# Column sums of an 8192 x 8192 matrix: the first block of rows laid out by halves, and three small TensorE sums moved around the second strip

One core of a Trainium2 chip. The metric is the device time of one execution in microseconds, the median over runs.

## The reference

```python
def setup_inputs():
    return {"x": np.random.randn(8192, 8192).astype(np.float32)}   # 268.4 MB

def reference(x):
    return np.sum(x, axis=0)                                        # 8192 numbers
```

## The kernel before

The rows come in 32 blocks of 256 (8 MiB each, two rows per partition). VectorE folds 31 blocks into a running sum. The last block is summed as six parts of its first 128 rows ("halves") and six strips of its other 128 rows, the strips getting narrower. TensorE reduces halves, strips and VectorE's carry over the partitions with a matmul by ones. ScalarE and VectorE copy the sums out of PSUM, and three stores write them.

```python
    G = NBUF * P * K                                   # P 128, K 2, NBUF 3
    xg = x[0 : near // NBUF * G, :].rearrange(
        "(g p b k) c -> g b p k c", p=P, b=NBUF, k=K)  # 30 blocks, interleaved in threes
    xn = x[near * P * K : last * P * K, :].rearrange("(p k) c -> p k c", k=K)
    xl = x[last * P * K :, :].rearrange("(k p) c -> k p c", p=P)
    # ... cut: tiles, semaphores
    def piece_sums(src, n, start, sem=None, val=0):    # 4 matmuls, one per 32 PSUM partitions
    # ... cut
        for t in range(last):
            i = nc.sync.dma_start(out=bufs[t % NBUF][:],
                in_=xn if t == near else xg[t // NBUF, t % NBUF])
            if t >= NBUF:
                i._wait_ge(s_free, t - NBUF + 1)
            i.then_inc(s_buf[t % NBUF], 16)
    # ... cut: two loads of halves, six of strips, each strip with its own semaphore
        half(0, s_half[0])
        half(1)
        carry_sums(0)
        carry_sums(1)
        half(2, s_half[1])
        strip_sums(0)
        strip_sums(1)
        carry_sums(2)
        for n in (3, 4, 5):
            half(n)
        strip_sums(2)
        carry_sums(3)
        strip_sums(3)
        carry_sums(4)
        carry_sums(5)
        strip_sums(4)
        strip_sums(5)
    # ... cut: six copies out of PSUM, three stores
```

Of the kernel before, what the change touches and what calls it, by code (L numbers as in the profile page):

```python
# [10 lines left out]
P = 128  # L11
K = 2
NBUF = 3
# [10 lines left out]
def kernel(  # L24
# [5 lines left out]
    nc = tc.nc  # L30
# [3 lines left out]
    near, last = T - 2, T - 1  # L34
# [1 line left out]



    G = NBUF * P * K
    xg = x[0 : near // NBUF * G, :].rearrange(  # L40
        "(g p b k) c -> g b p k c", p=P, b=NBUF, k=K
    )
    xn = x[near * P * K : last * P * K, :].rearrange("(p k) c -> p k c", k=K)
    xl = x[last * P * K :, :].rearrange("(k p) c -> k p c", p=P)

    pool = ctx.enter_context(tc.tile_pool(name="sb", bufs=1))
# [4 lines left out]
    bufs = [  # L51
        pool.tile([P, K, C], F32, name=f"buf{b}", tag=f"buf{b}") for b in range(NBUF)
    ]
# [19 lines left out]
    def rows(t, k, c0=0, w=None):  # L73
        return bufs[t % NBUF][:, k, c0 : C if w is None else c0 + w]
# [3 lines left out]
    def vadd(o, a, b, sem, val):  # L78

        nonlocal n_dve  # L80
        i = nc.vector.tensor_tensor(out=o, in0=a, in1=b, op=ADD)  # L81
        i._wait_ge(sem, val)
        i.then_inc(s_dve, 1)
        n_dve += 1
        return n_dve

    def piece_sums(src, n, start, sem=None, val=0):

        w, r = STRIPS[n], RUN[n]
        runs = src[:, START[n] : START[n] + w].rearrange(  # L90
            "p (u j i) -> p j u i", j=NJ, i=r
        )
        for j in range(NJ):
            i = nc.tensor.matmul(  # L94
                out=ps[n][32 * j : 32 * j + 32, 0 : w // NJ],
                lhsT=ones[:],
                rhs=runs[:, j],
                start=start,
                stop=True,
                skip_group_check=True,  # L100
            )
            if sem is not None and j == 0:
                i._wait_ge(sem, val)
        return i

    with tc.tile_critical(sync_engine=mybir.EngineType.DVE) as section:  # L106
        nc.gpsimd.memset(ones[:], 1.0).then_inc(s_one, 1)  # L107







        def take(sem, n):
            nc.vector.sem_inc(sem, -n)._wait_ge(sem, n)  # L116

        def block(b):
            r0, r1 = bufs[b][:, 0, :], bufs[b][:, 1, :]
            take(s_buf[b], 17)  # L120
            nc.vector.tensor_tensor(  # L121
                out=r0, in0=r0, in1=bufs[(b - 1) % NBUF][:, 1, :], op=ADD
            ).then_inc(s_op, 1)
            take(s_op, 1)
            nc.vector.sem_inc(s_free, 1)  # L125
            nc.vector.tensor_tensor(out=r1, in0=r1, in1=r0, op=ADD).then_inc(  # L126
                s_buf[(b + 1) % NBUF], 1
            )

        assert near % NBUF == 0  # L130
        take(s_buf[0], 16)
        nc.vector.tensor_tensor(  # L132
            out=rows(0, 1), in0=rows(0, 1), in1=rows(0, 0), op=ADD
        ).then_inc(s_buf[1], 1)
        for b in range(1, NBUF):
            block(b)
        with nc.vector.Fori(0, near // NBUF - 1):
            for b in range(NBUF):
                block(b)


        carry = {}
        for c0, parts in ((0, ((0, 2 * GROUP),)), (2 * GROUP, ((2, GROUP), (3, GROUP)))):
            w = 2 * GROUP
            d = vadd(
                rows(near, 0, c0, w),
                rows(near, 0, c0, w),
                rows(near - 1, 1, c0, w),
                s_buf[near % NBUF],
                17,  # L150
            )
            for g, gw in parts:
                v = vadd(
                    rows(near, 1, g * GROUP, gw),
                    rows(near, 1, g * GROUP, gw),
                    rows(near, 0, g * GROUP, gw),
                    s_dve,
                    d,
                )
                for i in range(gw // GROUP):  # L160
                    carry[g + i] = v


        for t in range(last):
            i = nc.sync.dma_start(out=bufs[t % NBUF][:], in_=xn if t == near else xg[t // NBUF, t % NBUF])
            if t >= NBUF:
                i._wait_ge(s_free, t - NBUF + 1)
            i.then_inc(s_buf[t % NBUF], 16)

        for h in range(2):  # L170
            c0, w = h * (C // 2), C // 2
            i = nc.sync.dma_start(out=rows(last, 0, c0, w), in_=xl[0][:, c0 : c0 + w])  # L172
            if h == 0:
                i._wait_ge(s_free, last - NBUF + 1)
            i.then_inc(s_half[h], 16)
        for n, w in enumerate(STRIPS):
            c0 = START[n]
            nc.sync.dma_start(  # L178
                out=rows(last, 1, c0, w), in_=xl[1][:, c0 : c0 + w]
            ).then_inc(s_strip[n], 16)  # L180



        def half(n, sem=None):
            piece_sums(rows(last, 0), n, True, sem, 16)

        def carry_sums(n):
            piece_sums(rows(near, 1), n, False, s_dve, carry[min(n, 3)])

        def strip_sums(n):  # L190
            piece_sums(rows(last, 1), n, False, s_strip[n], 16).then_inc(s_pe, 1)

        nc.tensor.wait_ge(s_one, 1)
# [3 lines that stand above are left out]
        carry_sums(1)  # L197
        half(2, s_half[1])
        strip_sums(0)
        strip_sums(1)  # L200
        carry_sums(2)
        for n in (3, 4, 5):
            half(n)
        strip_sums(2)
        carry_sums(3)
        strip_sums(3)
# [6 lines that stand above are left out]
        at = [START[n] // NJ for n in range(len(STRIPS))]  # L213
        for n in range(len(STRIPS)):
            w = STRIPS[n] // NJ
            o, p = res[:, at[n] : at[n] + w], ps[n][:, 0:w]
            c = nc.vector.tensor_copy(out=o, in_=p) if n in (3, 5) else nc.scalar.copy(o, p)  # L217
            c._wait_ge(s_pe, n + 1)
            c.then_inc({3: s_three, 5: s_end}.get(n, s_act), 1)

        lanes = slice(0, 32 * (NJ - 1) + 1, 32)

        def store(eng, n0, n1, sem, val):
            c0, c1 = START[n0], START[n1] + STRIPS[n1]
            return eng.dma_start(
                out=out[c0:c1].rearrange("(u j i) -> j u i", j=NJ, i=RUN[n0]),
                in_=res[lanes, c0 // NJ : c1 // NJ].rearrange(
                    "j (u i) -> j u i", i=RUN[n0]
                ),
            )._wait_ge(sem, val).then_inc(s_out, 16)  # L230

        store(nc.sync, 0, 2, s_act, 3)
        store(nc.sync, 3, 3, s_three, 1)
        nc.sync.wait_ge(s_act, 4)
        store(nc.sync, 4, 5, s_end, 1)
# [42 lines left out]
```

## Time and profile before

| | value |
|---|---|
| time | 627.25 us, median of 3 runs (627.19 to 627.32) |
| span of the profiled execution | 625.6 us (this execution took 627.52) |
| DMA | busy in all slices, 268.44 MB read |
| VectorE | 531.2 us busy, idle for a while in each block |
| TensorE | 13.2 us busy, all of it after 607 us |

The prediction shows the lines. A timeline line gives start, length, engine, source line, operation, names, shapes and count, then in brackets the idle time before it and what ended that. In the listing of transfers the last number is the time from issue to landing.

### The profile page before, as it was taken

To read this page: it belongs to the slowest core of one execution; us is meant where nothing else is said; L and a number is where in the kernel's file an instruction comes from. 1 tells how busy PE (TensorE), PEld (TensorE's weight loads), DVE (VectorE), ACT (ScalarE), POOL (GpSimd) and SP (SyncE) were. 2 spreads that over 40 slices of the span, in tenths; PEclk is the share of its full clock that TensorE was granted. 3 is DMA by queue.
4 is the path that set the end of the run, shared out by engine and by line. 5 is a ranking of instruction groups with operands and counts; after the bars stand their busy time and mean duration, and the time that the engine had idled before them with its cause. 6 is when DMAs were issued, how large, how long until landed. Compare 5 with 4: busy or idle time off the path is not lost. (4 is left out here: it accounts for less than half of the span.)

```text
span 625.6 us, 571 instructions
## 1 busy us (share of the span) xinstructions
PE 13.2 (2%) x144; PEld 4.1 (1%) x144; DVE 531.2 (85%) x66; ACT 3.4 (1%) x5; POOL 0.3 (0%) x5
## 2 busy tenths in 40 slices
PE   0000000000000000000000000000000000000016
PEld 0000000000000000000000000000000000000002
DVE  0538988889888899888898888988889888899887
ACT  0000000000000000000000000000000000000001
POOL 0000000000000000000000000000000000000000
PEclk9999999999999999999999999999999999999999
DMA  9999999999999999999999999999999999999997
GB/s 402 402 469 402 465 406 465 406 465 406 448 423 432 440 419 453 402 469 402 469 402 469 402 469 402 465 406 465 406 465 406 453 419 432 440 423 448 402 435 306
DMA packets 5661, 268.49 MB, mean 429 GB/s; under 512 B 652, under 2 KB 784, under 8 KB 1052
## 3 DMA queue, kind: packets, MB, share of 16 engines
q1 hardware_dynamic: 5660, 268.47, 99.2%
q8 instruction: 1, 0.02, 0.0%
HBM read 268.44 MB, written 0.03 MB: 429 GB/s over the span
## 5 line engine op out<-in xcount | busy, mean ns | idle before, releaser
L121 DVE TENSOR_TENSOR buf<-buf,buf 128x8192 f32<-128x8192 f32 x29 | 252.1, 8693 | 58.1 <-DVEq L116 58.1
L126 DVE TENSOR_TENSOR buf<-buf 128x8192 f32<-128x8192 f32 x29 | 252.1, 8693 | 6.9 <-DVEq L116 6.9
L132 DVE TENSOR_TENSOR buf<-buf 128x8192 f32<-128x8192 f32 x1 | 8.7, 8691 | 23.1 <-DVEq L116 23.1
L94 PE MATMUL ps<-buf,ones 128*32 128x512 f32 (+3 forms) x144 | 13.2, 513 | 609.5 <-DMA buf<-in_x_dram 609.1
L81 DVE TENSOR_TENSOR buf<-buf,buf 128x4096 f32<-128x4096 f32 x2 | 8.8, 4422 | 1.6 <-DMA buf<-in_x_dram 1.6
L81 DVE TENSOR_TENSOR buf<-buf 128x2048 f32<-128x2048 f32 (+1 forms) x3 | 8.9, 3000 | 0.1
L94 PEld LDWEIGHTS ps<-buf,ones 128*32 128x32 f32 x144 | 4.1, 117 | 618.5 <-DMA buf<-in_x_dram 610.9
L217 ACT COPY res<-ps 128x512 f32<-128x512 f32 (+1 forms) x4 | 2.1, 520 | 618.7 <-PE ps L94 618.7
L217 DVE COPY res<-ps 128x256 f32<-128x256 f32 (+1 forms) x2 | 0.7, 325 | 2.0 <-PE ps L94 2.0
L217 ACT ACT_TABLE_LOAD x1 | 1.3, 1283 | 1.0 <-DVEq L106 1.0
L107 POOL MEMSET ones<- 128x32 f32 x1 | 0.1, 126 | 0.6 <-DVEq L106 0.6
L262 POOL MEMSET const-bfloat16-1.0<- 128x1 bf16 x1 | 0.1, 102 | 0.0
L262 POOL MEMSET const-uint8-127<- 128x1 uint8 x1 | 0.1, 102 | 0.0
L262 POOL MEMSET const-float32-0.0<- 128x1 f32 x1 | 0.1, 99 | 0.2 <-issue 0.2
L262 POOL MEMSET const-float32-1.0<- 128x1 f32 x1 | 0.1, 99 | 0.0
## 6 DMA issues: line engine op xcount, KB each, us to landing
buf<-in_x_dram SPq DMA_DIRECT2D x2, 2048.0 KB, 17.5
buf<-in_x_dram SPq DMA_DIRECT2D x3, 1024.0 KB, 23.6
buf<-in_x_dram SPq DMA_DIRECT2D x1, 512.0 KB, 26.4
buf<-in_x_dram SPq DMA_DIRECT2D x31, 29.7
buf<-in_x_dram SPq DMA_DIRECT2D x1, 384.0 KB, 26.8
buf<-in_x_dram SPq DMA_DIRECT2D x1, 128.0 KB, 26.7
out_dram<-res SPq DMA_DIRECT2D x2, 4.0 KB
out_dram<-res SPq DMA_DIRECT2D x1, 24.0 KB
```

What stands on the lines that cost most here:

```text
L81: i = nc.vector.tensor_tensor(out=o, in0=a, in1=b, op=ADD)
L94: i = nc.tensor.matmul(out=ps[n][32 * j : 32 * j + 32, 0 : w // NJ], lhsT=ones[:], rhs=runs[:, j], start=start, stop=True, skip_group_chec ...
L107: nc.gpsimd.memset(ones[:], 1.0).then_inc(s_one, 1)
L121: nc.vector.tensor_tensor(out=r0, in0=r0, in1=bufs[(b - 1) % NBUF][:, 1, :], op=ADD).then_inc(s_op, 1)
L126: nc.vector.tensor_tensor(out=r1, in0=r1, in1=r0, op=ADD).then_inc(s_buf[(b + 1) % NBUF], 1)
L132: nc.vector.tensor_tensor(out=rows(0, 1), in0=rows(0, 1), in1=rows(0, 0), op=ADD).then_inc(s_buf[1], 1)
L217: c = nc.vector.tensor_copy(out=o, in_=p) if n in (3, 5) else nc.scalar.copy(o, p)
L262: nc = _bacc.Bacc("TRN2", target_bir_lowering=False, num_devices=1)
```

## The change

The intent: start the stream with pieces that neighbouring partitions read next to each other, and do the half-row sums of strips 3 to 5 while TensorE waits for strips, not when it is late for strip 2.

```diff
-    G = NBUF * P * K
-    xg = x[0 : near // NBUF * G, :].rearrange(
-        "(g p b k) c -> g b p k c", p=P, b=NBUF, k=K
-    )
-    xn = x[near * P * K : last * P * K, :].rearrange("(p k) c -> p k c", k=K)
+    F = P * K
+    xf = x[0:F, :].rearrange("(k p) c -> p k c", p=P)
+    xg = x[F : last * F, :].rearrange("(g p b k) c -> g b p k c", p=P, b=NBUF, k=K)
...
-            i = nc.sync.dma_start(out=bufs[t % NBUF][:], in_=xn if t == near else xg[t // NBUF, t % NBUF])
+            rows_in = xg[(t - 1) // NBUF, (t - 1) % NBUF] if t else xf
+            i = nc.sync.dma_start(out=bufs[t % NBUF][:], in_=rows_in)
...
         strip_sums(0)
+        half(3)
         strip_sums(1)
+        half(4)
+        half(5)
         carry_sums(2)
-        for n in (3, 4, 5):
-            half(n)
         strip_sums(2)
```

## The prediction

> **What bounds the kernel now.** I read the page's first parts, then the chain of waits that ended last, then the timeline of the last 35 us, then the issue times of the last transfers with their times to landing.
>
> ```profile
> span 625.6 us, 571 instructions
> PE 13.2 (2%) x144; PEld 4.1 (1%) x144; DVE 531.2 (85%) x66; ACT 3.4 (1%) x5; POOL 0.3 (0%) x5
> ...
> DMA  9999999999999999999999999999999999999997
> ...
> L121 DVE TENSOR_TENSOR buf<-buf,buf 128x8192 f32<-128x8192 f32 x29 | 252.1, 8693 | 58.1 <-DVEq L116 58.1
> L126 DVE TENSOR_TENSOR buf<-buf 128x8192 f32<-128x8192 f32 x29 | 252.1, 8693 | 6.9 <-DVEq L116 6.9
> ```
>
> The DMA row is full in 39 of 40 slices. VectorE works 8.69 + 8.69 us per 8 MiB block plus short gaps and then waits (58.1 us over 29 blocks, 10.6 of them before block 1), so it is not the bound. The first L121 add starts at 42.44 and the first L81 add, which the landing of block 30 released, at 602.62: (602.62 - 42.44) / 29 = 19.317 us per 8.389 MB block, or 434 GB/s. The transfer of each block is issued long before it can begin (29.7 us median from issue to landing against 19.3 us of moving), so the queue is never empty between the first packet and the last. Whatever shifts the start of the stream, or lengthens it anywhere, shifts the end by as much. Only two ends are not transfer: the start-up (issue at 0.97, first add at 23.15: 22.18 us, 2.9 us over a block's 19.3) and the tail. The tail in the timeline, from different stretches of it:
>
> ```profile
> 615.88 4.50 DVE L81 TENSOR_TENSOR buf<-buf 128x2048 f32<-128x2048 f32 x2
> ...
> 617.26 5.49 PE L94 MATMUL ps<-buf,ones 128*32 128x512 f32 x96 [1.39 <-DMA buf<-in_x_dram]
> 618.22 0.16 PEld L94 LDWEIGHTS ps<-buf,ones 128*32 128x32 f32 x8 [0.80 <-DVE buf L81]
> ...
> 621.95 0.43 DVE L217 COPY res<-ps 128x256 f32<-128x256 f32 x1 [1.57 <-PE ps L94]
> 622.71 0.32 ACT L217 COPY res<-ps 128x192 f32<-128x192 f32 x1 [1.04 <-PE ps L94]
> 622.82 0.22 DVE L217 COPY res<-ps 128x64 f32<-128x64 f32 x1 [0.45 <-PE ps L94]
> ```
>
> From 617.26 to the end TensorE runs without a break: the 96 matmuls carry no later wait. So at the very end TensorE, not the arrival of data, sets the pace, and it is late against the data. How late comes from the landings of the last strips (numbered 0 to 5):
>
> ```profile
> 593.61 23.61 DMA buf<-in_x_dram
> ...
> buf<-in_x_dram SPq DMA_DIRECT2D x1, 1024.0 KB, 25.6
> buf<-in_x_dram SPq DMA_DIRECT2D x1, 512.0 KB, 26.4
> ...
> buf<-in_x_dram SPq DMA_DIRECT2D x1, 384.0 KB, 26.8
> buf<-in_x_dram SPq DMA_DIRECT2D x1, 128.0 KB, 26.7
> ```
>
> Issues follow each other by 0.475 us: strip 1 at 593.61, strip 2 at 594.08, then 594.55, 595.03 and 595.50 for strips 3, 4 and 5. With 25.6, 26.4, 26.8 and 26.7 to landing: strip 1 lands at 617.22, strip 2 at 619.7, strip 3 at 620.95, strip 4 at 621.83, strip 5 at 622.2. In the timeline strip 2's sums start only at 619.97, strip 3's at 621.26, strip 4's at 622.13 and strip 5's, the last matmuls, at about 622.46. Each is 0.25 to 0.3 us after its landing, where an unblocked start follows a landing by about 0.04 us (617.22 to 617.26).
>
> [...] the last block's two half-row transfers (16 KB pieces) land 4.87 us apart for 2.097 MB (592.66 + 19.7 against 592.29 + 15.2), while a quarter of a 64 KB-piece block takes 19.317 / 4 = 4.83. [...] blocks read at a 192 KB pitch per partition, and the block at 64 KB and the last block at 32 KB, all keep 418 to 437 GB/s.
>
> **The change part by part.**
>
> (a) Order of TensorE in the tail. Nothing is added or removed: 144 matmuls before and after, the same 18 groups. `half(3)` (8 matmuls, 0.43 us) moves in front of strip 1, `half(4)` and `half(5)` (0.32 + 0.11 us) between strip 1 and `carry_sums(2)`. Before, all three (0.86 us, from 619.11 to 619.97) stood between `carry_sums(2)` and strip 2. A 512-column group takes 0.86 us, read from the starts.
> - `half(2)` ends at 614.43, strip 0 starts at 614.81 and its matmuls are fed by 615.7. `half(3)` takes 615.7 to 616.1. Strip 1 lands only at 617.22, so it falls wholly into the 1.39 us idle stretch: free.
> - Strip 1 is fed by 618.12. `half(4)` and `half(5)` take until 618.57. `carry_sums(2)`, which VectorE freed at 618.17 (615.88 + 2.29), starts 0.36 us later than before, and is through at 619.43. Strip 2 lands at 619.7, so this delay is free too.
> - Strip 2 then starts at 619.7 + 0.05 = 619.77 in place of 619.97: 0.20 us gained. From there the order is as before and has no hole if nothing else binds: `carry_sums(3)` at 620.63 (VectorE done at 615.88 + 4.50 = 620.38), strip 3 at 621.06 (landed 620.95), strip 4 at 621.93 (landed 621.83), strip 5 at 622.25 (landed 622.2). All are ready, the last by only 0.05 us. The last matmuls, the two last copies and the last store move 0.20 us earlier with them. More than about 0.21 cannot be had, as strip 5 lands at 622.2.
>
> Sum of (a): -0.20 us.
>
> (b) First block. Before, each partition reads one 64 KB piece; now two 32 KB pieces, 4 MB apart. 128 packets more, 8 more on each of the 16 engines. From the comparison above, 6 more packets per engine cost 4.87 - 4.83 = 0.04 us, so about 0.007 us each (an estimate that charges the extra semaphore write to them as well); 8 of them cost +0.06 us. They delay the whole stream, as it never idles.
>
> (c) Start-up. The issue-to-first-add time has 2.9 us of latency in it[...]. Neighbouring partitions' first pieces were 192 KB apart and will be 32 KB apart. I have no measured basis for a sign and take 0, give or take 0.25 us; it passes to the end in full.
>
> (d) The other 30 blocks shift by 256 rows and the block before the last joins the interleaving. Its interval (583.42 to the landing wait that ended at 602.62, 19.2 us between add starts) is no different from the others, so 0.
>
> VectorE's adds have the same shapes and count; nothing changes there: 0. Total: -0.20 + 0.06 + 0 = -0.14 us, or 627.25 - 0.14 = 627.11, rounded to 627.1.
>
> **The rivals.**
> - The stream's start moves. For it: the 2.9 us of start-up, and that every later landing hangs on it. If the new layout opens faster, up to -0.3 us more: about 626.8. If the 256 smaller pieces delay the first packets, +0.3: about 627.4. This is the largest uncertainty.
> - Address conflict in the first block. [...] Halving the rate in one block would add 19 us: 646. Against it: the last block is read with exactly this row-per-partition pitch at full rate. I give it below 1%.
> - TensorE's gain is swallowed: VectorE frees `carry_sums(3)` at 620.38 and strips 4 and 5 land within 0.1 us of when TensorE would want them. If part (b) makes everything land 0.06 later, the gain over those landings stays the same, since VectorE and strips shift together. If the wait in front of strips 4 or 5 adds a tenth, the gain is 0.1 and the time 627.2.
> - Later delivery of `carry_sums(2)` delays strip 2. Slack is 0.3 us (619.43 against 619.7), so this needs slower matmuls than those of the same minute[...].
>
> **Range and chances.** The measured runs of before lie within 0.13 us. With start-up (0.25), tail (0.1) and the scatter (0.1) taken as independent, the spread is about 0.28, and 8 in 10 needs 1.28 times that, 0.36: 626.7 to 627.5, widened slightly. Two per cent is 12.5 us, out of reach for the tail, and only the address conflict could make it slower by that much.
>
> **What would show it.** Right: one PE break in front of strip 2 with a wait on DMA, near 619.8; strip 5's matmuls within 0.1 us of its landing; 128 more packets; all L119 and L124 adds at 8.69 us; the first VectorE add at 23.2, give or take 0.25. Wrong: a first add outside that, an interval of blocks other than 19.3 us, or a PE break before strips 3 to 5 that eats the 0.20 us.

The charge in (b) is an estimate from the trace's 4.87 and 4.83 us, shared evenly over 16 DMA engines. Even sharing fits the changed kernel's records: 256 pieces of 32 KB, each 1.213 us in the median, make 256 x 1.213 / 16 = 19.4 us, a block's time. What the 2.9 us of the start-up consist of was not shown. The rival of an address conflict is a bare supposition, its halved rate, 646 us and 1% included. What speaks against it is measured: the last block's 8.389 MB took 19.63 us by the records (602.29 to 621.92, the ends of block 30's and strip 5's last 4-byte packets), which is 427 GB/s against the 434 of the blocks before it.

## The result

The changed kernel took 627.54 us (median of 6 runs: 627.22, 627.35, 627.53, 627.55, 628.75, 628.84). The kernel before took 627.29 (6 runs, 627.19 to 627.49). The ratio is 1.0009, with a 95% interval of 0.9996 to 1.0022: the same. Ratios are the mean time of one kernel's fast runs over that of the other's of the same rounds, so not quite the ratio of the medians quoted. The forecast of "within 2%" held. The median lies 0.04 us above the range, and two runs lie 1.3 us above it. All runs counted as fast, as 1.3 us is only 0.2%.

The changed kernel's page shows the same work and 128 packets more:

```profile
span 625.8 us, 571 instructions
...
DMA packets 5789, 268.49 MB, mean 429 GB/s; under 512 B 652, under 2 KB 784, under 8 KB 1052
...
L119 DVE TENSOR_TENSOR buf<-buf,buf 128x8192 f32<-128x8192 f32 x29 | 252.1, 8692 | 58.6 <-DVEq L114 58.6
L130 DVE TENSOR_TENSOR buf<-buf 128x8192 f32<-128x8192 f32 x1 | 8.7, 8693 | 22.9 <-DVEq L114 22.9
```

The first add waited 22.9 us, not 23.1: the stream opened 0.23 us earlier. The tail, from the changed kernel's timeline:

```profile
602.91 4.43 DVE L79 TENSOR_TENSOR buf<-buf,buf 128x4096 f32<-128x4096 f32 x1 [1.57 <-DMA buf<-in_x_dram]
...
620.07 0.16 PEld L92 LDWEIGHTS ps<-buf,ones 128*32 128x32 f32 x8 [1.05 <-DMA buf<-in_x_dram]
...
622.54 0.17 PEld L92 LDWEIGHTS ps<-buf,ones 128*32 128x32 f32 x8 [0.16 <-DMA buf<-in_x_dram]
622.83 0.32 ACT L217 COPY res<-ps 128x192 f32<-128x192 f32 x1 [1.04 <-PE ps L92]
622.94 0.23 DVE L217 COPY res<-ps 128x64 f32<-128x64 f32 x1 [0.45 <-PE ps L92]
```

TensorE now waits for strip 2 (620.07) and for strip 5 (622.54): it is no longer late. (The brackets give the idle time of the weight loads. By the records the break between matmuls before strip 2 is just under 0.15 us, too short for the timeline to print.) The last strip lands at 622.50 (record of the trace) and its first matmul starts at 622.58, 0.08 behind; before it was 622.20 and 622.46, 0.26 behind. From the add that block 30 releases to the last copy it is 622.94 - 602.91 = 20.03 us, against 622.82 - 602.62 = 20.20. But block 30's add itself is 0.29 us later than before. That came in the middle. Three adds of the kernel before:

```profile
100.48 8.69 DVE L121 TENSOR_TENSOR buf<-buf,buf 128x8192 f32<-128x8192 f32 x1 [1.69 <-DVEq L116]
119.77 8.69 DVE L121 TENSOR_TENSOR buf<-buf,buf 128x8192 f32<-128x8192 f32 x1 [1.66 <-DVEq L116]
139.09 8.69 DVE L121 TENSOR_TENSOR buf<-buf,buf 128x8192 f32<-128x8192 f32 x1 [1.70 <-DVEq L116]
```

and the same three of the changed kernel:

```profile
100.36 8.69 DVE L119 TENSOR_TENSOR buf<-buf,buf 128x8192 f32<-128x8192 f32 x1 [1.82 <-DVEq L114]
119.67 8.69 DVE L119 TENSOR_TENSOR buf<-buf,buf 128x8192 f32<-128x8192 f32 x1 [1.69 <-DVEq L114]
139.25 8.69 DVE L119 TENSOR_TENSOR buf<-buf,buf 128x8192 f32<-128x8192 f32 x1 [1.96 <-DVEq L114]
```

The steps are 19.29 and 19.32 before, 19.31 and 19.58 after. VectorE is as fast as ever, and the waits in brackets are longer: the data came late. Over the whole stream, first add to block 30's, it is 579.99 us against 579.47: 0.52 lost. So in the profiled run: -0.23 (start) + 0.52 (stream) - 0.17 (tail) = +0.12 at the last copy. The two profiled executions still took 627.53 and 627.52: at the end of the profiled span the difference is 0.11 (625.75 against 625.64 by the records), so about 0.1 lies outside it, where no trace looks. The sum is good to a tenth at best. This leaves the two runs at 628.8, which the profiled one does not explain.

### The profile page after: what moved, and what is told of

Same layout as the page of the kernel before. It is cut to its first block, busy times and chain, and to the rows that moved or that the text cites. A ratio compares the mean times of both kernels' runs of the same rounds, so it can differ in the third digit from the quotient of the medians.

```text
span 625.8 us, 571 instructions
## 1 busy us (share of the span) xinstructions
PE 13.4 (2%) x144; PEld 3.9 (1%) x144; DVE 531.2 (85%) x66; ACT 3.4 (1%) x5; POOL 0.3 (0%) x5
## 5 line engine op out<-in xcount | busy, mean ns | idle before, releaser
L130 DVE TENSOR_TENSOR buf<-buf 128x8192 f32<-128x8192 f32 x1 | 8.7, 8693 | 22.9 <-DVEq L114 22.9
## 6 DMA issues: line engine op xcount, KB each, us to landing
buf<-in_x_dram SPq DMA_DIRECT2D x1, 384.0 KB, 26.8
buf<-in_x_dram SPq DMA_DIRECT2D x1, 128.0 KB, 26.7
```

The source lines that it names most:

```text
L130: nc.vector.tensor_tensor(out=rows(0, 1), in0=rows(0, 1), in1=rows(0, 0), op=ADD).then_inc(s_buf[1], 1)
```

## The experiments

Sixteen kernels, each timed in 5 rounds, in four groups of four that shared a chip and the runs of the kernel before. All results were correct. "Slow" below means a run over 628 us, split_all aside, whose packets alone cost 1 us. The layout of the change has two parts: "shift" moves the 30 blocks by 256 rows, "split" reads the first block in two pieces per partition.

| run | layout | order | other | five times, sorted, us |
|---|---|---|---|---|
| tail_only | before | new | | 627.07 627.07 627.09 627.13 627.46 |
| shift_only | shift alone | new | | 627.04 627.10 627.13 627.14 628.50 |
| split_only | split alone | new | | 627.07 627.28 628.56 628.76 629.03 |
| both_again | new | new | | 626.93 627.04 627.06 627.28 629.25 |
| after_32_more | new | new | 32 instructions more | 628.42 628.46 628.64 628.65 628.66 |
| before_32_more | before | before | 32 more | 627.12 627.26 627.29 627.55 629.03 |
| after_32_fewer | new | new | 32 fewer | 627.05 627.06 627.23 627.24 627.53 |
| layout_only | new | before | | 627.20 627.21 627.32 627.77 627.78 |
| order_32_fewer | before | new | 32 fewer | 627.24 627.25 627.25 627.30 627.32 |
| fewer_again | new | new | 32 fewer | 627.01 627.06 627.07 627.10 627.51 |
| shift_32_fewer | shift alone | new | 32 fewer | 627.25 627.25 627.26 627.26 627.32 |
| split_all | all split | new | 32 fewer | 628.05 628.14 628.21 628.22 628.77 |
| before_64_more | before | before | 64 more | 628.13 628.34 628.35 628.39 628.98 |
| both_third | new | new | | 627.02 627.20 627.33 628.78 629.14 |
| order_again | before | new | | 626.94 627.30 627.34 627.36 627.38 |
| after_16_fewer | new | new | 16 fewer | 627.05 627.15 627.17 627.17 627.45 |

The kernel before, over all groups: 42 runs, median 627.28, 41 of them from 627.16 to 627.57 and one at 628.91.

### First group: which part of the change

The first theory was that the stretch of slow blocks belongs to the layout (its shift, or its split first block), the rival that it is chance.

tail_only is the kernel before with the TensorE lines of the diff alone:

> Only the new TensorE order, with the row layout of before. In all theories the tail gives its 0.18 to 0.20 us: 627.05 to 627.1 against 627.25, the last strip's matmuls under 0.1 us behind its landing, the first add at 23.15 as before. If the slow stretch between 80 and 200 us of the changed kernel (about 0.5 us lost to block intervals of 19.45 to 19.58 in place of 19.32) belongs to the layout, none of it is seen here, and no run is over 627.5. If it is chance (another kernel's or another chip's noise), block intervals over 19.42 and runs near 628.8 appear here as well.

Measured: median 627.09, no run over 627.5. From block 30's add (602.51) to the last copy (622.53) it is 20.02 us, so the tail's gain is there without the layout. Its stream took 579.48.

shift_only is the changed kernel with

```diff
-    xf = x[0:F, :].rearrange("(k p) c -> p k c", p=P)
+    xf = x[0:F, :].rearrange("(p k) c -> p k c", k=K)
```

> The changed kernel, but the first block with 64 KB pieces, so that only the shift of the interleaved 30 blocks by 256 rows is left of the layout. Theory that the shifted addresses cause the slow stretch: intervals over 19.42 between 80 and 200 us, 627.3 to 627.6, and some runs near 628.8. Theory that the first block's pieces (their start and the offsets between DMA engines that they leave) cause it: intervals of 19.27 to 19.39 throughout, 627.0 to 627.15.

Measured: four runs at 627.04 to 627.14, and no slow stretch beyond 60 us. The shifted addresses are not its cause. But the fifth run took 628.50, and it was the profiled one. Its stream took 579.57, as in the others. The time went in the last two microseconds. TensorE in the timeline, and then the last two strips in the listing of transfers:

```profile
617.10 5.18 PE L92 MATMUL ps<-buf,ones 128*32 128x512 f32 x80 [0.99 <-DMA buf<-in_x_dram]
623.57 0.32 PE L92 MATMUL ps<-buf,ones 128*32 128x64 f32 x8 [1.28 <-DMA buf<-in_x_dram]
...
buf<-in_x_dram SPq DMA_DIRECT2D x1, 384.0 KB, 26.9
buf<-in_x_dram SPq DMA_DIRECT2D x1, 128.0 KB, 28.2
```

Strip 4 took its usual 26.9 us. Strip 5 took 28.2 in place of 26.7, and TensorE sat idle 1.28 us for it. By the records of its landing, fifteen of the sixteen counts of its semaphore, one from each DMA engine as I read it, were in by 622.00 and one at 623.52. For that one, the packet of 4 bytes that counts the semaphore up started only at 622.43. (In the kernel before, the last such packet of strip 5 ends at 621.92, and the last count comes at 622.20.) What held it up is in the queues of the 0.1 us from 621.45 to 621.55 (packets that start there, MB, their time as a share of the 16 engines'):

```profile
q8 instruction: 1, 0.02, 58.2%
q1 hardware_dynamic: 18, 0.02, 44.8%
```

The page calls queue q8 "instruction", and I take what it moves for a fetch of instructions: one packet of 16,384 bytes from 621.51 to 622.44 (0.93 us). The late packet started in its last 0.02 us and ended 0.01 us after it. The records do not name an engine; that the two shared one is read from these times. The fetch's 0.93 us is also not the whole loss: the late packet landed 1.1 us after its start, where the fifteenth took 0.29 (621.71 to 622.00). Every profile here has exactly one such fetch in the tail; the page of before counts it too (queue q8, one packet, 0.0%), and I had passed over it.

In 15 of the 18 profiles taken in all, the fetch did not make the run slow. This run took 1.4 us more than its others. What let the fetch go first, the records do not show.

Offsets between the engines, which the expectation takes to come from the first block's pieces, are in the records of the pair: in the kernel before, the sixteen 4-byte packets of a block (one from each engine, as I read it) end 0.67 to 0.72 us apart, from first to last, in every one of 31 blocks; in the changed kernel 0.39 to 0.52. That it is the pieces that leave them was not shown.

split_only moves the split first block to the rows ahead of the last block, so that the 30 blocks keep their old addresses:

```diff
-    xf = x[0:F, :].rearrange("(k p) c -> p k c", p=P)
-    xg = x[F : last * F, :].rearrange(...)
+    xf = x[near * F : last * F, :].rearrange("(k p) c -> p k c", p=P)
+    xg = x[0 : near * F, :].rearrange(...)
```

> The changed kernel, but the first block takes its rows (in two 32 KB pieces per partition, as in the change) from just ahead of the last block, and the interleaved 30 blocks keep the addresses of before. Theory that the first block's pieces cause the slow stretch: first add about 0.2 us earlier than 23.15, then intervals over 19.42 somewhere in the first 200 us, 627.3 to 627.6 and a scatter of over 1 us. Theory that the shifted addresses cause it: the early first add is kept, intervals 19.27 to 19.39, 626.8 to 626.9.

Measured: three of five runs slow, and the scatter that I had expected, but not for the reason given: the profiled run (627.07) lost only 0.1 us in its stream, and the slow runs' 1.5 to 2.0 us over it are nearer to the 1.4 of the delayed strip than to the 0.5 of a slow stretch.

> The changed kernel itself once more, for its scatter. If the slow stretch is a property of this kernel: median 627.3 to 627.6, at least one run in six over 628, and again block intervals over 19.42 in the first 220 us, perhaps elsewhere than before. If it was chance: median 626.85 to 627.0, no run over 627.3.

Measured: one slow run, and the other four at 626.93 to 627.28. The run at 626.93 was profiled: first add at 22.88, stream 579.47, tail 622.34 - 602.35 = 19.99. That is the predicted course, with both gains and no loss. The slow stretch is thus no fixed property of the kernel.

### Second group: is it the fetch?

The theory now: TensorE's sequencer asks for its next block at a fixed place in its program. The new order brings that place forward against the landings, and now and then the request comes before one DMA engine has taken its last input packets. No record shows the request; this is a guess to be tested. The rivals: chance, the store, or the layout alone. The test changes only how many instructions TensorE has. after_32_more and before_32_more add, to the changed kernel and to the kernel before:

```diff
         nc.tensor.wait_ge(s_one, 1)
+        for _ in range(8):
+            nc.tensor.matmul(out=ps[5][0:32, 0:32], lhsT=ones[:], rhs=ones[:],
+                             start=True, stop=True, skip_group_check=True)
```

> The changed kernel with 8 tiny dummy matmuls ahead of everything on TensorE: 32 instructions more in its program (each fp32 matmul is two weight loads and two passes), done at 1 us, where nothing waits for them. Theory that the slow runs of about 628.5 are made by TensorE's instruction fetch (one 16 KB packet of 0.93 us in the instruction queue) that overtakes the last strip's final packet on one of the 16 DMA engines, and that it is asked for when TensorE reaches a fixed place in its program: the fetch now starts about two groups (0.6 to 0.9 us) earlier, before 621.0, always ahead of that engine's last packets; every run slow, 627.9 to 628.7. Theory that the slow runs have another cause (a late transfer by chance, the store on the same queue): the 32 instructions change nothing, most runs 626.9 to 627.3 and one in three at 628.5.

Measured: five of five slow, 628.42 to 628.66. The fetch started at 621.10, while strip 4 was still coming, and strip 4 landed late as well (28.1 us from issue, against 26.8). A cause by chance or by the store is out: the first store was issued at 621.73, after the fetch. (The dummies were done at 2.24 us rather than 1: TensorE's next matmul, at 607.76, had 605.52 us of idle time before it. Two weight loads and two passes for each matmul call is what the page of before shows: 144 of each for 72 calls.) Nor is it the granted clock: four of these five runs have a mean of 1.000, and so have 11 of the 21 slow runs. (Three of the longer ones have 0.997: 629.03 of before_32_more, 628.98 of before_64_more and 628.91 of the kernel before. There the clock may have added something; no profile shows it.)

> The kernel before with the same 8 dummy matmuls, neither layout nor order changed. Fetch theory: the kernel before gets slow runs as well, though it never had one in 18 runs: at least three of five at 628.0 to 629, the fetch starting earlier than 621.53. If the new layout or the new order itself makes the slow runs: all runs at 627.2 to 627.5 as without the dummies.

Measured: one of five slow (629.03), not three: a miss, and not clear of the one in 42 of the kernel before. The fetch of the profiled run started at 621.38, 0.16 earlier than in the kernel before, and still just after its engine had finished. By the theory, then, 32 were too few here; before_64_more below tests that.

after_32_fewer sums the halves of strips 3 to 5 as one group of 512 columns in a bank of its own. ScalarE copies that out early, and VectorE adds it:

```diff
-        half(3)
+        half_rest()          # columns of strips 3, 4 and 5 -> psh, 4 matmuls
         strip_sums(1)
-        half(4)
-        half(5)
...
+            if n > 2:        # hs: ScalarE's copy of psh
+                c = nc.vector.tensor_tensor(out=o, in0=p, in1=hs[:, h0 : h0 + w], op=ADD)
```

> The changed kernel with 32 TensorE instructions fewer: the halves of strips 3, 4 and 5 are summed as one group of 512 columns into a bank of their own, which ScalarE copies out early, and VectorE adds that copy where it copied before. Fetch theory: the fetch starts later than the last strip's landing (622 or later) or not at all; no slow run in five, 626.9 to 627.2 apart from chance losses in the stream of up to 0.5. Other causes: slow runs as often as in the changed kernel, one in three.

Measured: no slow run, as the fetch theory had it. But the fetch started at 621.52, not after 622. The records say why its start moves so little: in 14 of the 18 profiles taken in all it starts within 4 ns of the end of a 4-byte packet of the input queue, itself 0.34 us behind another such packet. I read that as one engine ending strip 4 and strip 5, and then at once the fetch. The fetch mostly waits in line behind the input on its engine, so its start shows when that engine was done, not when the request came. Of the other four, three are slow runs (fetch first), and in one the fetch started after all input was in.

layout_only is the changed kernel with the TensorE order of before:

> The new row layout with TensorE's order of before. If the order alone brings the fetch forward against the landings: no slow run, and a median of 627.0 to 627.2, the earlier start of the stream (first add 0.2 us sooner) being the gain. If the layout alone is enough, since it brings the slowest DMA engine closer to the others: one or two of five runs at 628.3 to 629.

That the slowest engine comes closer to the others shows in the pair's records, one profile of each: strip 5's last count came 0.24 us after the one before it in the kernel before (621.96, 622.20), 0.05 in the changed kernel (622.45, 622.50).

Measured: no slow run, so the layout alone does not bring the race on. But its median is 627.32, not 627.0 to 627.2. The two runs at 627.77 and 627.78 lost 0.5 us in the stream (profiled: first add 22.90, stream 579.99).

### Third group: the layout without the race

order_32_fewer, fewer_again and shift_32_fewer carry the edit of after_32_fewer on three layouts. split_all is fewer_again with `"(g b k p) c -> g b p k c"` for the 30 blocks, so that every block comes in 32 KB pieces.

> The row layout of before, the new order, and the 32 TensorE instructions fewer that took the instruction fetch out of the tail. No fetch, no slow run. 627.0 to 627.15 in most runs, like the new order alone. If the new layout's first block is what makes the stream lose up to 0.5 us in some runs, at most one of five is over 627.3 here; if such losses are chance, two of five may be, as in the kernel before (8 of its 24 runs were 0.25 or more over its fastest).

> The new layout, new order and 32 instructions fewer once more, on the same chip as its three relatives. No slow run. If the layout's earlier start (0.2 us) is kept to the end: fastest run 626.85 to 627.0 and median at or under 627.05. If its stream loses more often: median 627.2 again and at least two of five over 627.2.

> As the one before, but the first block in 64 KB pieces: the shift of the 30 blocks alone. If the split first block makes the losses, all five within 627.0 to 627.2; if the shifted addresses do, the same scatter up to 627.5 as with the split block.

Measured: no slow run in fifteen. The two layouts without a split block gave 627.24 to 627.32, steady, but above the 627.15 and 627.2 that I had as the upper ends. Nor had the fetch left the tail, as the first of these texts has it: it started at 621.57, 621.85 and 621.40. The edit lengthens the tail: VectorE now adds strips 4 and 5 one after the other, and from block 30's add to the end of the last output it is 20.41 us in order_32_fewer against 20.25 in order_again below. The split block gave 627.01 to 627.10 and one run of 627.51. So the split layout was mostly 0.18 faster on this chip, with a loss in one run. Of the 0.15 between the profiled runs of order_32_fewer and fewer_again only 0.05 is there at the last copy (622.67 and 622.62); the rest lies outside the span and is not explained.

> Every block in two 32 KB pieces per partition, not only the first: 30 times the suspected cost of the split. By the estimate of the prediction (0.007 us for each packet more on an engine, 8 a block) 0.06 us a block and 1.7 us in all: block intervals of 19.38 and 628.7 to 628.9. If the smaller packets cost nothing once the stream runs, intervals stay at 19.32 and the time at 627.1; if row-per-partition addresses collide, intervals of 20 us and more and a time over 645.

Measured: 628.05 to 628.22 and one of 628.77. First add to block 30's add took 580.57 us against 579.52 in fewer_again: 1.05 us in 30 blocks, 0.035 a block. The cost of smaller packets is real and about half of the 0.06 that the prediction charged. No address collision: the steps stay near 19.35 us.

### Fourth group: the kernel before, driven into the slow mode

> The kernel before with 64 more TensorE instructions (16 tiny matmuls at 1 us), layout and order untouched. Fetch theory: the request comes two groups earlier still, ahead of the last packets of its DMA engine in every run: fetch at 621.2 or earlier, five of five at 628.3 to 629.2. If something in the new layout or order is needed as well: 627.2 to 627.5 as with none.

Measured: five of five at 628.13 to 628.98, with layout and order untouched. The strips in the listing, then the queues of the 0.1 us from 620.4:

```profile
buf<-in_x_dram SPq DMA_DIRECT2D x1, 384.0 KB, 28.2
buf<-in_x_dram SPq DMA_DIRECT2D x1, 128.0 KB, 28.0
...
q1 hardware_dynamic: 14, 0.04, 98.9%
q8 instruction: 1, 0.02, 58.2%
```

The fetch starts at 620.48, 1.06 us earlier than in the kernel before, and strips 4 and 5 land 1.4 and 1.3 us late. Again the loss is more than the fetch's 0.93 us: of the six 3 KB packets of strip 4 that came behind it, the first three took 0.33, 0.33 and 0.2 us, where the others took 0.12. TensorE's instruction count alone makes the slow mode.

> The changed kernel a third time. By the rate so far (3 slow of 11) one or two of five at 628.5 to 629.3; the others between 626.9 and 627.55.

Measured: two slow of five. Over its three sets the changed kernel has 5 slow runs of 16, and the 11 others have a median of 627.22.

> The new order with the layout of before, again. If order alone is enough for the race at the rate of the changed kernel, one or two of five slow; if the layout is needed too (it makes the slowest DMA engine finish closer to the one that fetches), none, and 627.05 to 627.5.

Closer to the one that fetches is so in the pair's records by a little: strip 5's last 4-byte packet ended 0.38 us after the start of the fetch in the kernel before (621.54, 621.92), 0.26 in the changed kernel (621.96, 622.22).

Measured: no slow run; the new order alone now has 0 of 10, median 627.2.

> The changed kernel with 16 TensorE instructions fewer: only the halves of strips 3 and 4 share a bank and are added by VectorE, strip 5 keeps its own and is copied by ScalarE beside it. Fetch theory: few or no slow runs, as the request comes one group later. Tail: strips 4 and 5 leave in parallel again, so about 0.1 us faster than with 32 fewer: most runs 626.9 to 627.0, apart from stream losses. If the two copies do not overlap: 627.07 as with 32 fewer.

Measured: no slow run, 627.05 to 627.45. The tail was 20.27 us (602.48 to the end of the last output, 622.75), shorter than with 32 fewer, but the profiled run lost about 0.15 in the stream and the median of 627.17 missed the 626.9 to 627.0. With 16 or 32 fewer no run of 25 was slow (split_all left aside); with the new order and all its instructions 9 of 36 were (the three sets of the changed kernel, tail_only, order_again, shift_only and split_only). That fits the theory but does not isolate the count, as the edits also change how strips 3 to 5 are summed and copied out. No version beats the kernel before by more than its interval: the lowest ratio is that of fewer_again, 0.9995, with an interval of 0.9981 to 1.0008.

## Why the prediction was wrong

- **Part (a), the tail, was right in mechanism and size.** Predicted -0.20. By the two points of the timeline it was -0.17 in the first profile, -0.18 in tail_only and -0.21 in both_again. The break in front of strip 2 and the 0.1 us lag of strip 5 came as described.
- **The failed step is in (a) as well: it took the landings as given.** "All are ready, the last by only 0.05 us" let TensorE run earlier with the data staying where it was. But TensorE's program also times a transfer, a fetch of 16 KB of instructions: with 64 TensorE instructions more and nothing else changed, it began at 620.48 in place of 621.54. By the times of the late packet in shift_only it shares a DMA engine with the input. In the profile before, as I read the 4-byte packets, the fetch started only when its engine had finished the input (621.54). With the new order on the new layout 5 of 16 runs were slow. None of these five was profiled; in the profiled slow run of shift_only, which has the same order, the fetch went ahead of strip 5's last packet and the strip landed after 28.2 us in place of 26.7. No rival in the prediction names this. Without its two slow runs the first set has a median of 627.44 (between 627.35 and 627.53), inside the range; with them it is 627.54.
- **The scatter was mis-sized.** The prediction took 0.1 us from three runs of the kernel before. Its 41 runs that were not slow span 0.41 us, and the 11 of the changed kernel 0.62 (626.93 to 627.55). The distance that is left from 627.1 to the first set's 627.44 is this scatter, of which the profiled run shows 0.52 us lost in the stream. Over all three sets the median of the runs that were not slow is 627.22, 0.1 from the prediction.
- **Part (c), the start, was set to 0 with the right size of doubt.** The eight profiles without a split first block have first adds from 22.81 to 23.20 (mean 23.01), the nine that split only the first block 22.84 to 22.95 (mean 22.90). The profile that I predicted from had 23.15, one of the late ones, 0.14 over that mean: so much of the 0.23 us seen in the pair need not come from the layout. By the prediction's own sign (23.2, give or take 0.25) the 22.92 of the changed kernel falls just outside.
- **Part (b) was half its charge:** 0.035 us a block, not 0.06, or 0.0044 for each packet more on an engine, not 0.007 (both shared evenly over 16 engines). The 4.87 against 4.83 that it was read from stood on landing times printed to 0.1 us, so that it came this near is luck.
- **The stream itself, taken as fixed, was not,** and the prediction's sign of being wrong, an interval other than 19.3 us, came true (19.58). First add to block 30's add: 579.42 to 579.57 in the eight profiles without a split first block (mean 579.48), 579.47 to 579.99 in the nine with it (mean 579.70; three near 579.99). In the bad ones, most of the packets in flight are slow at the same moments (around 126 to 131 us in the changed kernel, where 27 of 32 packets of 64 KB took longer than usual, 2.51 us on average against 2.42), at other moments in other runs. That speaks against one unlucky engine. Whether the split block makes such spells likelier, or whether it is chance and the chips used, these few profiles do not settle. It stays open.
- **"Same" was right,** since the rival with an address collision did not occur: split_all has one row per partition in every block, at steps near 19.35 us. No run here has a pitch from partition to partition outside 32 to 192 KB.

What is shown: more instructions on TensorE alone cause the slow mode in both kernels (five of five with 32 more in the changed kernel, five of five with 64 more in the kernel before). What is argued: that each unprofiled slow run, all five of the changed kernel among them, is the same event (1.3 to 1.5 us fits; the largest, 2.3 us above its kernel's fastest, would need a loss in the stream as well). What is open: why the new order was slow with either part of the new layout (9 of 26 runs) and not with the layout of before (0 of 10). The numbers are small, and in the profiles nothing but the moment of the request, which they do not record, would tell.

## What to carry to other kernels

Where transfers bound a kernel, as here (a block every 19.32 us, the DMA row full in 39 of 40 slices), everything that rides with them belongs in the account, also the instruction fetches. One of 0.93 us here cost 1.05 to 1.4 us of kernel time (before_64_more 628.35 against 627.30 of the kernel before on that chip; shift_only 628.50 against its others' 627.04 to 627.14). Find when each falls, and whether a change to an engine's program brings it forward into the last transfer. A change worth 0.2 us needs more than three runs of the old kernel as its yardstick, and a look at single runs for a second mode before a median is trusted. To test for this cause, add a few idle instructions at the program's start: if the slow mode becomes the rule, the program's length is in it.
